# Decay gates from one product of 96 stacked rows in place of a plain float32 product of 16 rows

## The chip, the core and the metric

The kernel runs on one core of a Trainium2 chip. The metric is the device time of one execution in microseconds (us); less is better. Each kernel's time is the median of several runs, and one further execution was recorded by the hardware profiler. In the profile PE is TensorE's matmul, PEld its weight load, DVE VectorE, ACT ScalarE, POOL GpSimd, and SP the engine whose queue issues the DMAs.

## What is computed

A block of a streaming encoder on 1024 tokens of 1024 channels, with 16 meta tokens ahead of them, all in float32: a norm, one wide projection, a pooling mixer and a chunked gated linear attention side by side, a gated merge, an output projection, and an MLP with a squared ReLU. The part that matters here is the decay gate of the attention. `lr` is the slice of 16 channels of the projection (`GLA_GATE_RANK`), and there are 256 key channels:

```
log_a = jax.nn.log_sigmoid((lr @ w_gate_up + b_gate).astype(jnp.float32)) / GLA_TAU
...
b = jnp.cumsum(ac, axis=2)
decay = jnp.exp(-jnp.abs(b[:, :, :, None, :] - b[:, :, None, :, :]))
```

So the product in question is (1024 + 16 tokens) x 16 by 16 x 256. It is small beside the other products, but its result goes through an exponential of a running sum.

## The kernel before, in words

**Operands.** The large products are split. An operand x is kept as a high part hi (x rounded to the matmul type `float32r`, written by ACT) and a low part lo = x - hi (written by DVE, also as `float32r`), and a product is the sum of three matmuls, hi*hi, hi*lo and lo*hi (`mm3`, lines 280 to 282, called line by line L280, L281, L282). The gate product alone is different: line 506 multiplies plain float32 operands, `wgu` (16 rows x 256, the gate weights) and the transposed `lr` (16 rows x 512 tokens, kept in the first 16 rows of the tile `gB`; 16 x 16 for the meta tokens, in `lrT_meta`).

**Order of the work.** PE's order is the order of the code. ACT, DVE, POOL and SP each run one queue in order too, but what stands where in it is decided by a scheduler when the program is built. The steps around the change are: `start` (norms, transposes and the value projection `v_tile`, whose weights lie in the tiles `vw`; at its end `lr_turn`, which transposes `lr` on PE and copies it out of PSUM on ACT), `pool_open` (frees the tiles of `start` and opens those of the next stage), and then, by the list at the end of `differences`, a0, d0, a1, d1, m0, a2, m1, a3, m2, k0, m3. Here a(g) is `a_block(g)`, the projection of pooling group g, 72 matmuls and three evacuations on ACT (L555); d(p) is `decays(p)`, the gate for half p of the key channels: three gate products (tokens 0 to 511, tokens 512 to 1023, meta), and for each ACT adds the bias while it takes the product out of PSUM (L507), then does absolute value, exponential and logarithm (L508 to L510), DVE finishes (L511), and ACT exponentiates (L520) before the result is stored; m(g) is `mix_block(g)`, the pooling sums on DVE, their split into `ph` (L574, L575), and six matmuls.

**PSUM banks.** Products go to banks that are handed out in turn by tag. `ms` has three banks. `lr_turn` takes all three, d0 takes all three, d1 takes all three, and m0 takes the next one for its first product, that is the bank that d1's first product had. A bank can be written again when its reader is done; for a gate product the reader is ACT's L507. The projections use the three banks of the tag `mm`.

**Weights of the projections.** `W1` is a ring of two slots. As soon as the last matmuls of a block have read a slot, ACT and DVE split the weights of the block after the next into it (L84, L85); the scheduler puts these ahead of the evacuations of the gate products in ACT's queue.

**Later.** In the merge (steps `yb_block` and `out_tile`, from about 460 us on) SP's queue loads gate and pooling rows (L1029, into tiles `o`, `t` and `c`) and weights (L118, through the staging tiles `raw`), DVE multiplies and adds them (L1080, L1081), and ACT and DVE split the result (L1084, L1085).

Of the kernel before, what the change touches and what calls it, by code (L numbers as in the profile page):

```python
# [7 lines left out]
F32 = mybir.dt.float32  # L8
F32R = mybir.dt.float32r
U8 = mybir.dt.uint8  # L10
ACT = mybir.ActivationFunctionType
ALU = mybir.AluOpType
AX = mybir.AxisListType

P = 128
D = 1024
SEQ = 1024
META = 16
KT = D // P
HALF = 512  # L20
# [76 lines left out]
class Raw:  # L97
# [11 lines left out]
    def load(self, ap, n):  # L109
        while any(self.slots[self.n % len(self.slots)] is t for t in self.held):  # L110
            self.n += 1
        self.last = self.slots[self.n % len(self.slots)]
        dst = self.last[:, :n]
        self.n += 1
        view = dst
        if len(ap.shape) == 3:
            view = dst.rearrange("p (a b) -> p a b", a=ap.shape[1])
        self.nc.sync.dma_start(view, ap)  # L118
        return dst
# [3 lines left out]
def kernel(  # L123
# [3 lines left out]
    nc = tc.nc  # L127
# [3 lines left out]
    w_gate_up, b_gate, gla_norm, w_gla_out, w_out = w_gate_up[0], b_gate[0], gla_norm[0], w_gla_out[0], w_out[0]  # L131
    norm_ffn, w_ff1, w_ff2 = norm_ffn[0], w_ff1[0], w_ff2[0]

    act, dve, pool, pe = nc.scalar, nc.vector, nc.gpsimd, nc.tensor
    left, right = Stack(tc, "left"), Stack(tc, "right")
# [18 lines left out]
    def bank(tag):  # L154
        if tag == "sc":
            sc_n[0] += 1
            return two("sc")[:, sc_n[0] % 2]
        return psp[tag].tile([P, 512], F32, name=f"b_{tag}", tag=tag)

    def two(tag):  # L160

        if tag in ("sc", "gs"):
            if tag not in wide:
                wide[tag] = psp[tag].tile([P, 2, 512], F32, name=f"b_{tag}", tag=tag)
            return wide[tag]
        return psp[tag].tile([P, 2, 512], F32, name=f"b_{tag}", tag=tag)
# [17 lines left out]
    gB = left.push("gB", [P, D], F32)  # L184
# [10 lines left out]
    stat = [tiny(16) for _ in range(4)]  # L195
    eps_t = tiny(1)
    pool.memset(eps_t, EPS)
    wgu = left.push("wgu", [16, 256], F32)
    metab = left.push("metab", [P, 5, 16], F32)
    lrT_meta = left.push("lrT_meta", [16, META], F32)  # L200
    raw = Raw(nc, [left.push(f"raw{i}", [P, D], F32) for i in range(2)])
    W1 = Ring(tc, raw, left.push("w1h", [P, 2, D], F32R), left.push("w1l", [P, 2, D], F32R), 2)
    left_ff = left.mark()
# [8 lines left out]
    def f32(ap):  # L212
        return ap.bitcast(F32)

    def col(v, n):
        return v.rearrange("(h p) -> p h", p=P)
# [87 lines left out]
    S, rings = {}, [W1]  # L304
# [44 lines left out]
    def buffer(key, depth, size=HALF, side=None):  # L349
        S[key] = (side or left).push(key, [P, depth, size], F32)  # L350
        S["n" + key], S["d" + key] = 0, depth

    def nxt(key):
        i = S["n" + key]
        S["n" + key] += 1
        return S[key][:, i % S["d" + key]]

    def halves():
        return [slice(h * HALF, (h + 1) * HALF) for h in range(2)]
# [3 lines left out]
    def ask_vw(i):  # L363
        vw_raw[i] = [
            raw.load(w_cols(C_V + i * 256 + j * P), D).rearrange("p (k c) -> p k c", k=KT) for j in range(2)
        ]
# [35 lines left out]
            nc.sync.dma_start(v_dram[i, t], o)  # L402

    def lr_turn():
        b = bank("ms")
        pe.transpose(b[:16, :16], S["lrtok"][:16, 8], ident[:16, :16])
        act.activation(lrT_meta, b[:16, :16], ACT.Copy)
        for h in range(2):
            b = bank("ms")
            for t in range(4):  # L410
                pe.transpose(b[:16, t * P : (t + 1) * P], S["lrtok"][:, 4 * h + t], ident)
            act.activation(gB[:16, h * HALF : (h + 1) * HALF], b[:16], ACT.Copy)


    SPREAD = {
# [7 lines left out]
    def start():  # L423
        act.preload_act_table_set("natural_log_exp_and_others")
        xs = left.push("xs", [P, 4, D], F32)
        us = left.push("us", [P, 3, D], F32)
        S["lrtok"] = left.push("lrtok", [P, 10, 16], F32)
        S["lrraw"] = left.push("lrraw", [P, KT, 16], F32)
        xm = left.push("xm", [META, D], F32)
        um = left.push("um", [META, D], F32)  # L430
        mf = left.push("mf", [P, 6, CH], F32)
        S["xr"] = right.push("xr", [P, KT, SEQ], F32)
        S["vw"] = [right.push(f"vw{i}", [P, 2, KT, n], F32R) for i, n in enumerate((VP, 256))]
        buffer("vo", 3, 2 * P, right)
        load = lambda t: nc.sync.dma_start(xs[:, t % 4], x[t * P : (t + 1) * P, :])
        blank = S["xr"].rearrange("p k c -> p (k c)")[:, -640:]
        pool.memset(blank, 0.0)

        def warm(n, cols=HALF):
            for _ in range(n):  # L440
                pe.matmul(bank("ms")[:, :cols], blank[:, HALF:], blank[:, :cols], start=True, stop=True)

        load(0)
        nc.sync.dma_start(um[:1], norm_mix[None, :])
        nc.sync.dma_start(ident, ident_in)
        ask_vw(0)
        nc.sync.dma_start(S["lrraw"], w_in[:, C_LR : C_LR + 16].rearrange("(k p) c -> p k c", p=P))
        pool.memset(xm[:1, :P], 1.0)
        warm(2)
        for c in halves():  # L450
            b = bank("mm")
            pe.matmul(b, xm[:1, :P], um[:1, c], start=True, stop=True)
            dve.tensor_copy(gB[:, c], b)
        warm(2)
        for t in range(8):
            if 0 < t < 6:
                load(t + 2)
            if t == 1:
                nc.sync.dma_start(xm, meta)
            if t == 3:  # L460
                W1.top_up()
            u = us[:, t % 3]
            layer_norm(xs[:, t % 4], u)
            transposed(u, t // 4, OFF[t // 4] + (t % 4) * P, ("ms", "sc"))
            if t == 0:
                load(1)
                load(2)
                warm(10, P)
                load_vw(0)
                ask_vw(1)  # L470
            if t == 6:
                layer_norm(xm, um)
            if t == 1:
                warm(6, P)
            if t == 2:
                load_vw(1)
            if t < 3:
                v_tile(0, t)
            else:
                for i, n in SPREAD[t]:  # L480
                    v_tile(i, n)
        transposed(um, 0, 0)
        v_tile(0, 7)
        v_tile(1, 6)
        v_tile(1, 7)
        v_tile(0, 8)
        v_tile(1, 8)
        lr_turn()
        nc.sync.dma_start(mf, masks)
        pool.tensor_copy(mask, mf)  # L490
        nc.sync.dma_start(pscale, col(pool_scale, 4))
        nc.sync.dma_start(bgate, col(b_gate, 2))
        nc.sync.dma_start(gnorm, col(gla_norm, 4))
        nc.sync.dma_start(wgu, w_gate_up)

    one = []
    step(one, start)


# [3 lines left out]
    def log_decay(lrT, p, n, y, t):  # L503

        b = bank("ms")[:, :n]
        pe.matmul(b, wgu[:, p * P : (p + 1) * P], lrT, start=True, stop=True)
        act.activation(y, b, ACT.Identity, bias=bgate[:, p : p + 1])  # L507
        act.activation(t, y, ACT.Abs)  # L508
        act.activation(t, t, ACT.Exp, scale=-1.0)
        act.activation(t, t, ACT.Ln, bias=1.0)  # L510
        dve.scalar_tensor_tensor(y, y, 0.0, t, ALU.min, ALU.subtract)  # L511

    META_LOG = (0, 3)

    def decays(p):
        def fn():
            for half, c in enumerate(halves()):
                y = nxt("c")
                log_decay(gB[:16, c], p, HALF, y, nxt("t1"))
                act.activation(y, y, ACT.Exp, scale=1.0 / TAU)  # L520
                nc.sync.dma_start(decay_dram[p, half], y)
                yield 0.6
            if p:
                act.activation(gnorm, gnorm, ACT.Copy, scale=0.5)
            log_decay(lrT_meta, p, META, metab[:, META_LOG[p]], metab[:, 4])
            if p:
                tc.keep_in_program_order(act.preload_act_table_set("exp_and_others"))

        return fn

    def pool_open():
        left.pop_to(base)
        right.pop_to(1)
        buffer("c", 4)
        buffer("t1", 3)
        S["left_t"] = left.mark()
        buffer("a", 2, 1056)
        buffer("s", 2, 1056)
        S["ph"] = left.push("ph", [P, 2, SEQ], F32R)
        mw = S["mw"] = left.push("mw", [P, 2, 4, P], F32R)  # L540
        r = raw.load(w_pool_mix.rearrange("g c e -> c g e"), 4 * P).rearrange("p (g e) -> p g e", g=4)
        act.activation(mw[:, 0], r, ACT.Copy)
        dve.tensor_tensor(mw[:, 1], r, f32(mw[:, 0]), ALU.subtract)

    step(one, pool_open)

    pooled = {}
# [1064 lines left out]
```

## Time and profile before

| | us |
|---|---|
| runs of the kernel | 1223.77, 1224.25, 1226.83 (median 1224.25) |
| profiled execution | 1226.16 |
| its span, first to last instruction | 1224.0 |
| PE busy in the span | 1209.7 |
| DVE busy | 841.4 |
| ACT busy | 574.3 |
| POOL busy | 75.8 |

The profiled execution's own time is 2.2 us above its span, and 1.9 us above the median of the runs. A row of the timeline gives start, duration, engine, line, operation, output<-inputs and how many instructions were merged; in brackets stand the idle time before and what ended it. Matmuls overlap: a matmul of 512 columns is shown with 0.39 us, but the next one starts 0.23 us later. So the cost of matmuls is read from the distance of their starts, not from their durations.

### The profile page before, as it was taken

The numbers are of one execution on the slowest core, as the hardware profiler recorded it, in microseconds if no ns is written. First come the engines' busy times: TensorE is split into PE (matmuls) and PEld (weight loads), VectorE is DVE, ScalarE is ACT, GpSimd is POOL, SyncE is SP. The second block draws the span as 40 slices with busy tenths as digits, with TensorE's granted clock in tenths as the row PEclk, the third lists the DMA queues.
The fourth block names the chain that finished last, engine by engine and source line by source line (L and its number), as shares of the span: only waits on it lengthen the run. The fifth ranks groups of instructions, "written<-read, shape, count | busy, mean of one in ns | idle before, by whom it ended". The sixth has DMA issues, their size and how long they took to land.

```text
span 1224.0 us, 18376 instructions
## 1 busy us (share of the span) xinstructions
PE 1209.7 (99%) x6807; PEld 998.3 (82%) x6807; DVE 841.4 (69%) x1383; ACT 574.3 (47%) x1011; POOL 75.8 (6%) x96
## 2 busy tenths in 40 slices
PE   9999999999999999999999999999999999999997
PEld 6988987778778887888778888888888888888886
DVE  6535657665777568835887676676775887887686
ACT  7627444444456223413655455454554444444544
POOL 0000043222230000000000000000000000000000
PEclk9999999999999999999999999999999999999999
DMA  8312334435238976921245354444569973333532
GB/s 236 93 40 95 118 100 130 146 105 164 82 135 269 336 242 217 322 93 53 109 138 167 129 172 146 157 155 135 176 223 328 333 251 100 100 95 95 169 96 88
DMA packets 154411, 193.80 MB, mean 158 GB/s; under 512 B 12209, under 2 KB 89281, under 8 KB 154322
## 3 DMA queue, kind: packets, MB, share of 16 engines
q1 hardware_dynamic: 154322, 192.64, 48.6%
q8 instruction: 53, 0.87, 0.3%
q14 instruction: 36, 0.29, 0.1%
HBM read 129.67 MB, written 62.93 MB: 157 GB/s over the span
## 4 chain that ended last, share of the span: by engine, by line
PE 91%; DVE 3%; DMA 2%; ACT 1%; issue 1%; POOL 0%; SPq 0%; DVEq 0%; POOLq 0%; ACTq 0%
PE b_mm L282 7%; PE b_mm L280 7%; PE b_mm L281 7%; PE b_y L280 6%; PE b_y L281 6%; PE b_y L282 6%; PE b_oa L282 5%; PE b_oa L280 5%; PE b_oa L281 5%; PE b_z L280 4%; PE b_z L281 4%; PE b_z L282 4%; PE b_sc L280 4%; PE b_ob L282 4%; PE b_ob L280 4%; PE b_ob L281 4%
## 5 line engine op out<-in xcount | busy, mean ns | idle before, releaser
L677 ACT ACTIVATE w1h<-raw 128x512 fp32r<-128x512 f32 x106 | 65.9, 622 | 59.4 <-PE b_y L281 25.3
L678 DVE TENSOR_TENSOR w1l<-raw,w1h 128x512 fp32r<-128x512 f32 x106 | 72.5, 685 | 21.9 <-ACT w1h L677 21.9
L280 PE MATMUL b_sc<-th,w1h 128*128 128x512 f32 x216 | 85.6, 396 | 0.5 <-ACT u2p L1395 0.5
L280 PE MATMUL b_z<-th,w1h 128*128 128x512 f32 x216 | 85.2, 395 | 0.2 <-DVE c L796 0.2
L281 PE MATMUL b_sc<-tl,w1h 128*128 128x512 f32 x216 | 84.9, 393 | 0.0
L281 PE MATMUL b_z<-tl,w1h 128*128 128x512 f32 x216 | 84.3, 390 | 0.4 <-DVE tl L1283 0.4
L677 ACT ACTIVATE w1h<-fs 128x512 fp32r<-128x512 f32 x81 | 51.1, 631 | 71.0 <-PE b_y L281 33.4
L282 PE MATMUL b_sc<-th,w1l 128*128 128x512 f32 x216 | 84.4, 391 | 0.0
L282 PE MATMUL b_z<-th,w1l 128*128 128x512 f32 x216 | 84.1, 389 | 0.0
L678 DVE TENSOR_TENSOR w1l<-fs,w1h 128x512 fp32r<-128x512 f32 x81 | 57.0, 704 | 26.6 <-ACT w1h L677 26.5
L280 PE MATMUL b_mm<-th,w1h 128*128 128x512 f32 (+1 forms) x208 | 72.1, 347 | 0.0
L281 PE MATMUL b_mm<-tl,w1h 128*128 128x512 f32 (+1 forms) x208 | 71.0, 342 | 0.0
L282 PE MATMUL b_mm<-th,w1l 128*128 128x512 f32 (+1 forms) x208 | 71.0, 341 | 0.0
L677 ACT ACTIVATE w1h<-bt 128x512 fp32r<-128x512 f32 x46 | 29.1, 632 | 70.8 <-issue 43.9
L1471 DVE TENSOR_TENSOR bt<-w,w 128x512 f32<-128x512 f32 x80 | 54.7, 684 | 0.4 <-DMA w<-in_w_ff_dram 0.4
L280 PE MATMUL b_mm<-wo,th 128*128 128x512 f32 x128 | 50.4, 394 | 0.0
L282 PE MATMUL b_mm<-wo,tl 128*128 128x512 f32 x128 | 49.9, 390 | 0.0
L281 PE MATMUL b_mm<-wo,th 128*128 128x512 f32 x128 | 49.8, 389 | 0.0
L280 PE MATMUL b_y<-wo,w1h 128*128 128x512 f32 x128 | 49.8, 389 | 0.0
L281 PE MATMUL b_y<-wo,w1h 128*128 128x512 f32 x128 | 49.8, 389 | 0.0
L282 PE MATMUL b_y<-wo,w1l 128*128 128x512 f32 x128 | 49.8, 389 | 0.0
L678 DVE TENSOR_TENSOR w1l<-bt,w1h 128x512 fp32r<-128x512 f32 x46 | 31.8, 691 | 25.6 <-ACT w1h L677 25.6
(405 smaller groups left out, 3342.7 us busy)
## 6 DMA issues: line engine op xcount, KB each, us to landing
hf_dram<-h SPq DMA_DIRECT2D x112, 256.0 KB, 2.1
raw<-hf_dram SPq DMA_DIRECT2D x112, 256.0 KB, 2.7
w<-in_w_ff_dram SPq DMA_DIRECT2D x64, 256.0 KB, 4.5
raw<-in_w_in_dram SPq DMA_DIRECT2D x22, 512.0 KB, 4.6
raw<-in_w_ff_dram SPq DMA_DIRECT2D x16, 512.0 KB, 4.2
rawx<-in_w_ff_dram SPq DMA_DIRECT2D x16, 512.0 KB, 4.2
rawp<-in_w_in_dram SPq DMA_DIRECT2D x10, 512.0 KB, 4.2
xs<-in_x_dram SPq DMA_DIRECT2D x8, 512.0 KB, 4.7
```

The source lines that it names most:

```text
L280: pe.matmul(ps, ah, bh, start=first and i == 0, stop=False, skip_group_check=more)
L281: pe.matmul(ps, ah, bl, start=False, stop=False, skip_group_check=more)
L282: pe.matmul(ps, al, bh, start=False, stop=last and i == n - 1, skip_group_check=more)
L677: act.activation(hi, a, ACT.Copy)
L678: dve.tensor_tensor(lo, a, f32(hi), ALU.subtract)
L1471: dve.tensor_tensor(bt, w, S["w2"][q[3:]][:, i], ALU.add if q[2] == "+" else ALU.subtract)
```

## The change

The gate product becomes one matmul in the split form, with the three terms laid under one another in the 128 rows of the array. Two new tiles of 96 rows are made, `lr` (96 x 1040) and `gu` (96 x 256), both `float32r`. In `lr`, rows 0 to 15 and 64 to 79 hold hi of the transposed `lr`, rows 32 to 47 hold lo. In `gu`, rows 0 to 15 and 32 to 47 hold hi of the gate weights, rows 64 to 79 hold lo. All other rows are zero. One product over the 96 rows is then hi*hi + lo*hi + hi*lo.

For this the weights are loaded three times into `wgu`, which now has 96 rows and is cleared by POOL at the start; `lr` is cleared by POOL; `stacked` writes hi twice on ACT and lo once on DVE for each of the three pieces; `gu` takes one ACT and one DVE instruction. `lr_turn` is called from `pool_open` and no longer from `start`. The tiles `lr` and `gu` lie where `vw` was.

```
-    wgu = left.push("wgu", [16, 256], F32)
+    wgu = left.push("wgu", [96, 256], F32)
...
-    lrT_meta = left.push("lrT_meta", [16, META], F32)
...
     def lr_turn():
+        def stacked(to, b):
+            act.activation(to[:16], b, ACT.Copy)
+            act.activation(to[64:80], b, ACT.Copy)
+            dve.tensor_tensor(to[32:48], b, f32(to[:16]), ALU.subtract)
+
         b = bank("ms")
         pe.transpose(b[:16, :16], S["lrtok"][:16, 8], ident[:16, :16])
-        act.activation(lrT_meta, b[:16, :16], ACT.Copy)
-        for h in range(2):
+        stacked(S["lr"][:, SEQ:], b[:16, :16])
+        for h, c in enumerate(halves()):
             b = bank("ms")
             for t in range(4):
                 pe.transpose(b[:16, t * P : (t + 1) * P], S["lrtok"][:, 4 * h + t], ident)
-            act.activation(gB[:16, h * HALF : (h + 1) * HALF], b[:16], ACT.Copy)
+            stacked(S["lr"][:, c], b[:16])
...
         pool.memset(blank, 0.0)
+        pool.memset(wgu, 0.0)
...
-        lr_turn()
         nc.sync.dma_start(mf, masks)
...
-        nc.sync.dma_start(wgu, w_gate_up)
+        for r in (0, 32, 64):
+            nc.sync.dma_start(wgu[r : r + 16], w_gate_up)
...
-        pe.matmul(b, wgu[:, p * P : (p + 1) * P], lrT, start=True, stop=True)
+        pe.matmul(b, S["gu"][:, p * P : (p + 1) * P], lrT, start=True, stop=True)
...
-                log_decay(gB[:16, c], p, HALF, y, nxt("t1"))
+                log_decay(S["lr"][:, c], p, HALF, y, nxt("t1"))
...
-            log_decay(lrT_meta, p, META, metab[:, META_LOG[p]], metab[:, 4])
+            log_decay(S["lr"][:, SEQ:], p, META, metab[:, META_LOG[p]], metab[:, 4])
...
     def pool_open():
+        right.pop_to(1)
+        S["lr"] = right.push("lr", [96, SEQ + META], F32R)
+        S["gu"] = right.push("gu", [96, 256], F32R)
+        pool.memset(f32(S["lr"]), 0.0)
+        lr_turn()
+        act.activation(S["gu"], wgu, ACT.Copy)
+        dve.tensor_tensor(S["gu"][64:96], wgu[64:], f32(S["gu"][64:96]), ALU.subtract)
         left.pop_to(base)
-        right.pop_to(1)
```

PE's order stays what it was, matmul for matmul; only the gate products read other tiles. At d1, PE stands so before (b_ms is a bank of the tag `ms`, th and w1l are operands of a1, ph and mw those of m0):

```order
L282 MATMUL b_mm<-th_144,w1l 128x512
L506 MATMUL b_ms<-gB,wgu 128x512 x2
L506 MATMUL b_ms<-lrT_meta,wgu 128x16
L280 MATMUL b_ms<-ph,mw 128x512
L281 MATMUL b_ms<-ph,mw 128x512
L282 MATMUL b_ms<-ph,mw 128x512
```

And now, where the lines of the code have moved (L506 is L511, L280 to L282 are L279 to L281):

```order
L281 MATMUL b_mm<-th_140,w1l 128x512
L511 MATMUL b_ms<-lr,gu 128x512 x2
L511 MATMUL b_ms<-lr,gu 128x16
L279 MATMUL b_ms<-ph,mw 128x512
L280 MATMUL b_ms<-ph,mw 128x512
L281 MATMUL b_ms<-ph,mw 128x512
```

The first matmul of m0, into a bank of `ms`, still stands right behind the three gate products of d1.

ACT's queue around `lr_turn` before (L542 splits the mix weights, L398 evacuates the last value tiles, L607 belongs to `differences`, L555 evacuates a0, L507 takes d0's gate products out of PSUM):

```order
L542 ACTIVATE mw<-raw_120 128x512
L398 ACTIVATE gB<-b_mm 16x256 x2
L407 ACTIVATE lrT_meta<-b_ms 16x16
L607 ACTIVATE t2h<-xr 128x2048
L412 ACTIVATE gB<-b_ms 16x512 x2
L555 ACTIVATE a<-b_mm 128x264 x2
L84 ACTIVATE w1h<-raw_124 128x1024
L555 ACTIVATE a<-b_mm 128x512
L507 ACTIVATE c<-b_ms,small 128x512 x2
```

And now:

```order
L542 ACTIVATE gu<-wgu 96x256
L397 ACTIVATE gB<-b_mm 16x256 x2
L405 ACTIVATE lr<-b_ms 16x16
L406 ACTIVATE lr<-b_ms 16x16
L618 ACTIVATE t2h<-xr 128x2048
L405 ACTIVATE lr<-b_ms 16x512
L406 ACTIVATE lr<-b_ms 16x512
L405 ACTIVATE lr<-b_ms 16x512
L406 ACTIVATE lr<-b_ms 16x512
L566 ACTIVATE a<-b_mm 128x264 x2
L84 ACTIVATE w1h<-raw_120 128x1024
L566 ACTIVATE a<-b_mm 128x512
```

Four instructions of ACT are added ahead of a0's first evacuation; behind it, through d1, L84 still stands ahead of the evacuation of the gate products.

Far from the change, in the merge, the scheduler's order of SP's queue comes out differently. Before (raw are staging tiles for weights, o and t the tiles of gate and pooling rows):

```order
L118 DMA raw_120<-in_w_gla_out_dram 128x4x256
L1029 DMA o<-gb_dram 128x512
L1029 DMA o<-ma_dram 128x512
L1029 DMA o<-gb_dram 128x512
L1029 DMA o<-ma_dram 128x512
L1029 DMA t_4717<-gb_dram 128x512
L1029 DMA t_4717<-ma_dram 128x512
L1029 DMA t_4717<-gb_dram 128x512
L1029 DMA t_4717<-ma_dram 128x512
L118 DMA raw_124<-in_w_gla_out_dram 128x4x256
```

And now:

```order
L118 DMA raw_116<-in_w_gla_out_dram 128x4x256
L118 DMA raw_120<-in_w_gla_out_dram 128x4x256
L1040 DMA t_4735<-gb_dram 128x512
L1040 DMA t_4735<-ma_dram 128x512
L1040 DMA t_4735<-gb_dram 128x512
L1040 DMA t_4735<-ma_dram 128x512
L1040 DMA o<-gb_dram 128x512
L1040 DMA o<-ma_dram 128x512
L1040 DMA o<-gb_dram 128x512
L1040 DMA o<-ma_dram 128x512
```

The second load of weights has moved ahead of the eight loads of rows, and the `t` loads ahead of the `o` loads. At d0 a few small rows of ACT and DVE have changed places; between d1 and the merge the order of ACT, DVE and SP is the same as before.

## Prediction, made before the changed kernel was run

> **What bounds the kernel now.** The page first: the span, the busy time of the engines and the shares of the chain that ended last.
>
> ```profile
> span 1224.0 us, 18376 instructions
> ...
> PE 1209.7 (99%) x6807; PEld 998.3 (82%) x6807; DVE 841.4 (69%) x1383; ACT 574.3 (47%) x1011; POOL 75.8 (6%) x96
> ...
> PE 91%; DVE 3%; DMA 2%; ACT 1%; issue 1%; POOL 0%; SPq 0%; DVEq 0%; POOLq 0%; ACTq 0%
> ```
>
> PE is idle for 14 of 1224 us, and 91% of the chain is PE. A microsecond taken from PE's queue is therefore worth a microsecond, if PE doesn't then stand still for something else. Next the chain in order of time, at the gate products (start, length, what):
>
> ```profile
> 91.50 2.04 PE b_ms L506 x6
> 105.07 2.04 PE b_ms L506 x6
> ```
>
> Both groups of gate products, d0 and d1, lie on the chain with 2.04 us each. PE's timeline at d0 and at d1 gives the finer picture:
>
> ```profile
> 90.66 0.39 PE L280 MATMUL b_mm<-th,w1h 128*128 128x512 f32 x1
> 90.89 0.39 PE L281 MATMUL b_mm<-tl,w1h 128*128 128x512 f32 x1
> 91.11 0.39 PE L282 MATMUL b_mm<-th,w1l 128*128 128x512 f32 x1
> 91.43 1.98 PE L506 MATMUL b_ms<-gB,wgu 16*128 16x512 f32 x4
> 93.25 0.28 PE L506 MATMUL b_ms<-lrT_meta,wgu 16*128 16x16 f32 x2
> 93.47 0.39 PE L280 MATMUL b_mm<-th,w1h 128*128 128x264 f32 x1
> 93.69 0.28 PE L281 MATMUL b_mm<-tl,w1h 128*128 128x264 f32 x1
> 93.81 0.28 PE L282 MATMUL b_mm<-th,w1l 128*128 128x264 f32 x1
> ...
> 104.46 0.39 PE L281 MATMUL b_mm<-tl,w1h 128*128 128x512 f32 x1
> 104.69 0.39 PE L282 MATMUL b_mm<-th,w1l 128*128 128x512 f32 x1
> 105.00 1.98 PE L506 MATMUL b_ms<-gB,wgu 16*128 16x512 f32 x4
> 106.83 0.29 PE L506 MATMUL b_ms<-lrT_meta,wgu 16*128 16x16 f32 x2
> 107.11 0.47 PE L280 MATMUL b_ms<-ph,mw 128*128 128x512 f32 x1
> ```
>
> A `float32r` matmul of 512 columns takes 0.225 us from start to start (90.66, 90.89, 91.11). A plain float32 product of 512 columns is two instructions; four of them and the first meta instruction fill 91.43 to 93.25, so one product costs about 0.86 us, nearly four times as much. It uses 16 rows of the array, and nothing in these rows says that fewer rows are cheaper.
>
> **The change, part by part.** *d0.* Without gate products the next matmul would start at 91.11 + 0.225 = 91.34; it starts at 93.47. The step costs 2.13 us. Now it is two products at 0.225 and one of 16 columns, for which I take 0.12, the distance at which matmuls of 264 columns follow each other (93.69, 93.81): 0.57 us. Bounds for that last one are 0 and 0.225. What follows is a1: its weights have been in the other slot since `start`, and its banks are of another tag. So d0 gives back 2.13 - 0.57 = 1.56, about 1.6 us (1.45 to 1.7).
>
> *d1.* The same sum at d1 is 107.11 - (104.69 + 0.225) = 2.20 us against 0.57, again 1.6 us on PE. But next is m0, which needs the bank of d1's first product. ACT's rows at d1:
>
> ```profile
> 104.89 1.06 ACT L84 ACTIVATE w1h<-raw 128x1024 fp32r<-128x1024 f32 x1 [2.38 <-PE b_mm L281]
> 105.85 0.58 ACT L555 ACTIVATE a<-b_mm 128x512 f32<-128x512 f32 x1
> 106.33 1.39 ACT L507 ACTIVATE c<-b_ms,small 128x512 f32<-128x512 f32 x2
> ```
>
> ACT starts the weights' split L84 when PE's last reader of that slot is done (the L281 from 104.46, shown to 104.85), then evacuates a1, and only then takes the gate product out: two L507 in 1.39 us, so the first is done at 106.33 + 0.69 = 107.02. PE's next start was 107.11, by its own sum and by ACT's alike: the two paths ended together. ACT's path hangs on the end of a1 and none of its three steps gets shorter, and its order at this place is unchanged. So m0 still starts 2.2 us behind the end of a1. How soon PE follows ACT is seen later, where it waits for ACT:
>
> ```profile
> 478.51 1.04 ACT L84 ACTIVATE w1h<-raw 128x1024 fp32r<-128x1024 f32 x1
> ...
> 479.61 0.50 PE L280 MATMUL b_mm<-yg,w1h 128*128 128x512 f32 x1 [2.33 <-ACT w1h L84]
> ...
> 480.94 0.80 PE L282 MATMUL b_mm<-yg,w1l 128*128 128x512 f32 x1 [0.60 <-DVE w1l L85]
> ```
>
> 478.51 + 1.04 to 479.61 is 0.06 us, so m0 could come at 107.08 instead of 107.11: a gain of 0.03, taken as 0. The new wait of about 1.6 us stands at m0's first matmul; behind it in PE's queue stand m0's other five and a2, and ACT and DVE wait for those. Its other operand, `ph`, comes from
>
> ```profile
> 100.68 0.69 DVE L575 TENSOR_TENSOR ph<-s,ph 128x512 fp32r<-128x512 f32 x1
> ```
>
> at 101.4, still ahead of 107.1 - 1.6 = 105.5.
>
> *Preparation.* ACT and DVE around `lr_turn`:
>
> ```profile
> 81.47 1.04 ACT L412 ACTIVATE gB<-b_ms 16x512 f32<-16x512 f32 x2
> 83.18 0.39 ACT L555 ACTIVATE a<-b_mm 128x264 f32<-128x264 f32 x1 [0.67 <-PE b_mm L282]
> ...
> 81.60 2.29 DVE L608 TENSOR_TENSOR t2l<-xr,t2h 128x2048 fp32r<-128x2048 f32 x1 [4.13 <-ACT t2h L607]
> 92.40 1.23 DVE L85 TENSOR_TENSOR w1l<-raw,w1h 128x1024 fp32r<-128x1024 f32 x1 [8.51 <-ACT w1h L84]
> ```
>
> ACT has four pieces of 512 in place of two, 1.04 us more, and a small one more; with 0.67 us free it delays a0's first evacuation by about 0.5 us, and that bank is next written in a1, at 92. The split of `gu`, one more, falls into ACT's idle time ahead of 79. DVE makes the low parts behind t2l (to 83.9), two of at most 0.69 us: done by 85.4. d0 needs them at 91.34, so 6 us cover them; and DVE has 8.5 us free there. Uncovered, all of it would cost 2.5 us. ACT's `gu` and POOL's clearing of `lr` must wait until `vw` has been read, by
>
> ```profile
> 76.05 0.29 PE L282 MATMUL b_mm<-vw,tl 128*16 128x272 f32 x1
> ...
> 0.77 0.63 POOL L437 MEMSET xr<- 128x640 f32 x1
> 33.83 0.50 SPq L494 DMA_DIRECT2D wgu<-in_w_gate_up_dram  x1
> ```
>
> at 76.34. POOL cleared 640 columns in 0.63 us, so 1040 take about 1.0: done at 77.4, two microseconds ahead of the transposes' evacuation at 79.6. Clearing `wgu` (0.25 us) stands at the start on an idle POOL. Two more DMA issues of 0.50 us each delay the weights of a2 on SP from 35.4 to 36.4, and a2's split reads them at 91. All this is counted at nothing.
>
> *Sum.* 1.56 + 0.03 + 0 = 1.6 us off. The profiled execution's 1226.16 would become 1224.6; it lies 1.9 above the median, and the median goes from 1224.25 to **1222.6**. Behind m0 I expect everything 1.6 us earlier in the same order, the merge apart.
>
> **The rivals.** *Both steps pay* (3.2 us, 1221.0): if ACT took d1's product out ahead of L84. The order says no; the bank's turn could be misread. 0.12.
>
> *The clock trips at m0.* Where PE had stood still, its clock was halved (granted clock is the column after POOL):
>
> ```profile
> 477.00:481.00 4.00, 1.07 (x5) 0.36 (x3) 4.00 (x7) 2.10 (x3) 0.00 (x0) 1.00 0.84 274
> 481.00:484.40 3.40, 3.40 (x8) 2.72 (x9) 1.78 (x3) 1.58 (x2) 0.00 (x0) 0.50 0.97 351
> 490.00:600.00 110.00, 109.50 (x504) 90.22 (x503) 66.21 (x112) 40.30 (x72) 0.00 (x0) 1.00 0.42 148
> ```
>
> Gaps of 2.33 and 0.60 us were followed by 3.4 us at 0.50, a loss of 1.7. A new gap of 1.6 might do the same: 1222.6 + 1.7 = 1224.3. [...] The trace thus speaks against leaning on it, but half as long a gap is milder: 0.13.
>
> *The wait at 477 shrinks.* It is fed by loads and stores whose landing varies, as in the answer on L1029:
>
> ```profile
> DMA to landing us min/median/max: 2.6/4.4/7.3
> ```
>
> If only the halved clock is escaped, 1222.6 - 1.7 = 1220.9; if the gaps go too, 2.9 more: 1218.0. The change does nothing for it. 0.10.
>
> *Slower: the moved loads of the merge.* Four loads into `o` now stand behind a load of weights and four into `t`:
>
> ```profile
> 489.92 1.22 DVE L85 TENSOR_TENSOR w1l<-raw,w1h 128x1024 fp32r<-128x1024 f32 x1
> ...
> 487.87 0.34 SPq L1029 DMA_DIRECT2D o<-gb_dram  x1
> 493.56 0.43 SPq L118 DMA_DIRECT2D raw<-in_w_gla_out_dram  x1
> ...
> 500.43 0.68 DVE L1080 SCALAR_TENSOR_TENSOR o<-o,b_mm 128x512 f32<-128x512 f32 x1
> ```
>
> The weights' staging tile is free at 491.2, so the first `o` load slips from 487.87 to about 493.6, and its reader runs at 500.43: 6.9 us, enough for the median landing and just short of enough for the slowest. But 0.5 MB and five loads of 0.26 MB, 1.8 MB, go out from 491.2; at the stage's mean of 148 GB/s they land at 503.4, 2.9 us late, and PE would wait for the bank: 1222.6 + 2.9 = 1225.5, slower. It decides against the kernel below 1.8 MB in 9.2 + 1.6 = 10.8 us, 167 GB/s; the queue ran at 274 and 351 where it was loaded, so 0.10.
>
> *The 96 rows cost as much as float32 before* (no gain, 1224.25): nothing speaks for it, as a `float32r` matmul of 128 rows has 0.225 us. 0.05.
>
> **How the numbers follow.** The forecast has 0.50. Runs differ by 3.1 us (1223.77 to 1226.83), so each case is smeared by about 1.5 us. The range 1219.8 to 1225.7 takes in forecast, both steps, clock, moved loads and no gain, and the nearer half of the shrunken wait. A measurement can tell about 0.3%, 3.7 us: faster means below 1220.6, which is the wait at 477 shrinking (0.10) and a third of both steps (0.04), 0.14 together. Slower means above 1227.9: a quarter of the moved loads and of the clock (0.06). Within 0.3%: 0.80.
>
> **What would show it.** Right: d0 takes about 0.6 us on PE; m0's first matmul shows an idle time of about 1.6 us that ACT's L507 ends (L512 there); a2 starts 1.6 us earlier than before, not 3.2; DVE's low parts are done by 86; the clock stays at 1.00 around 105. Wrong: m0 without a wait; a wait at d0; a clock of 0.50 behind m0; PE waiting for DVE or a DMA between 485 and 515; or a wait near 477 that has changed by more than a microsecond.

## The result and the profile after

| | us |
|---|---|
| before, 6 runs beside the changed kernel | 1225.46 median (1222.6 to 1226.86) |
| changed kernel, 6 runs | 1230.01 median (1229.53 to 1232.73) |
| ratio to before | 1.0044 [1.003, 1.0057] |
| profiled execution of the changed kernel | 1231.92, span 1230.0 |
| predicted | 1222.6 (1219.8 to 1225.7) |

The kernel became 0.44% slower, about 5 us, where 1.6 us of gain were forecast; the time lies above the range. The page of the changed kernel:

```profile
span 1230.0 us, 18382 instructions
...
PE 1212.6 (99%) x6801; PEld 997.0 (81%) x6801; DVE 843.9 (69%) x1387; ACT 576.1 (47%) x1015; POOL 77.1 (6%) x98
```

PE has six instructions fewer (the three gate products were x6 at d0 and at d1, and are x3 now) and is busy 2.9 us longer, and the span is 6.0 us longer, so PE's idle time grew by 3.1 us. The idle time is about that of three new waits, read below (1.50, 0.86 and 0.68 us). The busy time is the surprise: the gate products became about 3.2 us shorter, so the rest of PE's work takes about 6 us longer.

**The gate products.** PE's timeline of the changed kernel at d0 and d1 (L511 is the gate product, L279 to L281 the projections, before called L280 to L282):

```profile
90.77 0.39 PE L281 MATMUL b_mm<-th,w1l 128*128 128x512 f32 x1
90.99 0.64 PE L511 MATMUL b_ms<-lr,gu 96*128 96x512 f32 x3
91.49 0.37 PE L279 MATMUL b_mm<-th,w1h 128*128 128x264 f32 x1
...
102.69 0.39 PE L281 MATMUL b_mm<-th,w1l 128*128 128x512 f32 x1
102.91 0.64 PE L511 MATMUL b_ms<-lr,gu 96*128 96x512 f32 x3
105.06 0.50 PE L279 MATMUL b_ms<-ph,mw 128*128 128x512 f32 x1 [1.50 <-ACT c L512]
```

The three products of d0 take 91.49 - (90.77 + 0.225) = 0.50 us, where they took 2.13. At d1 they are as short, but m0 starts at 105.06, 2.14 us behind the end of a1 (2.20 before), after 1.50 us of waiting for ACT. ACT at the same place:

```profile
102.88 1.06 ACT L84 ACTIVATE w1h<-raw 128x1024 fp32r<-128x1024 f32 x1 [0.66 <-PE b_mm L280]
103.85 0.58 ACT L566 ACTIVATE a<-b_mm 128x512 f32<-128x512 f32 x1
104.33 1.26 ACT L512 ACTIVATE c<-b_ms,small 128x512 f32<-128x512 f32 x2
```

The chain is the one foretold: split of the weights, evacuation of a1, evacuation of the gate product, then m0. The preparation on ACT, DVE and POOL:

```profile
83.77 0.39 ACT L566 ACTIVATE a<-b_mm 128x264 f32<-128x264 f32 x1
...
83.81 1.28 DVE L407 TENSOR_TENSOR lr<-b_ms,lr 16x512 fp32r<-16x512 f32 x2
...
76.07 0.96 POOL L540 MEMSET lr<- 96x1040 f32 x1 [40.93 <-PE b_mm L281]
```

a0's first evacuation is 0.59 us later than before, the low parts are done at 85.09, and `lr` is cleared at 77.03; no PE wait follows from any of them. The step that the change is about does what was said of it.

**Where the time went.** Here are matmuls that stand in both kernels, from PE's timeline before:

```profile
93.47 0.39 PE L280 MATMUL b_mm<-th,w1h 128*128 128x264 f32 x1
...
485.15 0.39 PE L281 MATMUL b_mm<-yg,w1h 128*128 128x512 f32 x1
...
495.89 0.50 PE L280 MATMUL b_mm<-yg,w1h 128*128 128x512 f32 x1
...
631.23 0.47 PE L280 MATMUL b_z<-th,w1h 128*128 128x512 f32 x1
...
896.29 0.39 PE L282 MATMUL b_sc<-th,w1l 128*128 128x512 f32 x1
...
1203.20 0.39 PE L280 MATMUL b_oa<-w1h,fxh 128*128 128x512 f32 x1
```

and the same ones in the changed kernel (the first of them is the row at 91.49 above):

```profile
483.78 0.46 PE L280 MATMUL b_mm<-yg,w1h 128*128 128x512 f32 x1
...
495.63 0.51 PE L279 MATMUL b_mm<-yg,w1h 128*128 128x512 f32 x1 [0.86 <-DVE t L1091]
...
632.25 0.47 PE L279 MATMUL b_z<-th,w1h 128*128 128x512 f32 x1 [0.68 <-DVE h L1423]
...
898.60 0.39 PE L281 MATMUL b_sc<-th,w1l 128*128 128x512 f32 x1
...
1209.09 0.39 PE L279 MATMUL b_oa<-w1h,fxh 128*128 128x512 f32 x1
```

After minus before: -1.98, -1.37, -0.26, +1.02, +2.31, +5.89 us. Of the lead of 1.98 us behind d0, 0.35 was there ahead of d0. Between 178 and 350 us 0.7 us of it go, nearly all by 184 us, at two waits of 0.23 and 0.44 us that were 0 and 0.24 before. In the merge 1.1 us go at a new wait for DVE, and up to 632 us another 1.3, of which 0.68 is a further new wait. From 631 us on, through the MLP, the difference grows by 4.9 us without any wait. The windows view tells it in counts (two stretches of the MLP, first before, then after; the first number in brackets is PE's matmuls):

```profile
640.00:880.00 240.00, 240.00 (x1061) 198.72 (x1060) 169.34 (x265) 121.86 (x204) 0.00 (x0) 1.00 0.47 154
930.00:1200.00 270.00, 270.00 (x1192) 223.56 (x1192) 208.38 (x348) 122.06 (x223) 0.00 (x0) 1.00 0.51 165
```

```profile
640.00:880.00 240.00, 240.00 (x1055) 197.72 (x1055) 168.43 (x264) 120.68 (x201) 0.00 (x0) 1.00 0.47 154
930.00:1200.00 270.00, 270.00 (x1179) 220.87 (x1178) 205.85 (x340) 120.71 (x220) 0.00 (x0) 1.00 0.52 166
```

PE is never idle in either kernel, the granted clock is 1.00, and yet 6 and 13 matmuls fewer start in the same time. From the starts of single matmuls of 512 columns in the trace (distances above 260 ns left out): 226.7 ns apart before in both stages, now 227.8 ns from 620 to 900 us and 229.4 ns from 915 to 1210 us. About 1240 matmuls x 1.1 ns and 1300 x 2.7 ns make 1.4 + 3.5 = 4.9 us, the whole drift.

By operands, the slowest are those that take one operand from each side of the memory: tiles are pushed on a left side that grows upwards (`w1h`, `th`, `wo` and others) or a right side that grows downwards (`fxh`, `t4h`, `yg` and others). Pairs of `w1h` and `fxh` went from 226.3 to 233 ns; pairs of `wo` and `w1h`, both left, stayed at 226.7. But matmuls with both operands on one side have a part in it: in the last stage, behind each switch of sides, most of the first ten are slower (single ones up to 236 ns), and from the eleventh on they are back at 226 to 227. By the means, about 1.5 of the last stage's 3.5 us fall on them. The line of the diff that reaches them is the removal of `lrT_meta`, 16 columns of 4 bytes: it moved every left-side tile pushed behind it down by 64 bytes, and no right-side tile. In the built program `w1h` starts at byte 31616 of each partition before and at 31552 now, `fxh` at 219008 in both. By 256, the large operand tiles of both sides had the remainder 128 before; now the left ones have 64.

### The profile page after: what moved, and what is told of

Its sections match the earlier page's. It is cut to its first block, busy times and chain, and to the rows that moved or that the text cites. A ratio compares the mean times of both kernels' runs of the same rounds, so it can differ in the third digit from the quotient of the medians.

```text
span 1230.0 us, 18382 instructions
## 1 busy us (share of the span) xinstructions
PE 1212.6 (99%) x6801; PEld 997.0 (81%) x6801; DVE 843.9 (69%) x1387; ACT 576.1 (47%) x1015; POOL 77.1 (6%) x98
## 4 chain that ended last, share of the span: by engine, by line
PE 91%; DVE 4%; DMA 2%; issue 2%; ACT 1%; POOL 0%; SPq 0%; DVEq 0%; ACTq 0%; POOLq 0%
PE b_mm L279 7%; PE b_mm L281 7%; PE b_mm L280 7%; PE b_y L279 6%; PE b_y L280 6%; PE b_y L281 6%; PE b_oa L281 5%; PE b_oa L279 5%; PE b_oa L280 5%; PE b_z L279 4%; PE b_z L280 4%; PE b_z L281 4%; PE b_sc L279 4%; PE b_ob L279 4%; PE b_ob L281 4%; PE b_ob L280 4%
## 5 line engine op out<-in xcount | busy, mean ns | idle before, releaser
L279 PE MATMUL b_sc<-th,w1h 128*128 128x512 f32 x216 | 86.0, 398 | 0.7 <-ACT u2p L1406 0.5
L279 PE MATMUL b_z<-th,w1h 128*128 128x512 f32 x216 | 85.3, 395 | 1.1 <-DVE h L1423 0.7
L280 PE MATMUL b_sc<-tl,w1h 128*128 128x512 f32 x216 | 84.7, 392 | 0.0
L280 PE MATMUL b_z<-tl,w1h 128*128 128x512 f32 x216 | 84.3, 390 | 0.4 <-DVE tl L1294 0.4
L281 PE MATMUL b_sc<-th,w1l 128*128 128x512 f32 x216 | 84.7, 392 | 0.0
L281 PE MATMUL b_z<-th,w1l 128*128 128x512 f32 x216 | 84.1, 390 | 0.0
L279 PE MATMUL b_mm<-th,w1h 128*128 128x512 f32 (+1 forms) x208 | 72.0, 346 | 0.0
L280 PE MATMUL b_mm<-tl,w1h 128*128 128x512 f32 (+1 forms) x208 | 71.1, 342 | 0.0
L281 PE MATMUL b_mm<-th,w1l 128*128 128x512 f32 (+1 forms) x208 | 71.0, 341 | 0.0
L279 PE MATMUL b_mm<-wo,th 128*128 128x512 f32 x128 | 50.6, 395 | 0.0
L281 PE MATMUL b_mm<-wo,tl 128*128 128x512 f32 x128 | 50.1, 391 | 0.0
L280 PE MATMUL b_mm<-wo,th 128*128 128x512 f32 x128 | 49.8, 389 | 0.0
L279 PE MATMUL b_y<-wo,w1h 128*128 128x512 f32 x128 | 49.8, 389 | 0.0
L280 PE MATMUL b_y<-wo,w1h 128*128 128x512 f32 x128 | 49.8, 389 | 0.0
L281 PE MATMUL b_y<-wo,w1l 128*128 128x512 f32 x128 | 49.8, 389 | 0.0
```

The costliest lines, as they stand in the source:

```text
L279: pe.matmul(ps, ah, bh, start=first and i == 0, stop=False, skip_group_check=more)
L280: pe.matmul(ps, ah, bl, start=False, stop=False, skip_group_check=more)
L281: pe.matmul(ps, al, bh, start=False, stop=last and i == n - 1, skip_group_check=more)
```

## The experiments

Two losses were to be explained, the drift and the merge, and a gain that stays behind the wait at m0. The theory: the drift comes from the distance between the addresses of the two operands, the merge from another order there, and neither from the gate product. The rival: something in the new step (its tiles, its work on ACT, DVE, POOL or SP) slows PE later on.

**e1: the 64 bytes put back.**

```
     metab = left.push("metab", [P, 5, 16], F32)
+    left.push("fill", [P, 16], F32)
```

> The changed kernel with an unused tile of 64 bytes per partition in the place of the tile lrT_meta that the change took away, so that every tile behind it has its address of before again; the scheduler's order in the merge is then the one of before too. Address theory (the loss comes from the 64 bytes by which the tiles of the left side moved): matmuls of 512 columns are 226.7 ns apart again in both parts of the MLP (they were 227.8 and 229.4 in the changed kernel), no PE wait near 495, m0's wait of 1.5 us stays, and the time is 1.6 us below the kernel before (1.0 to 2.2). Rival (the loss comes from the stacked product itself or from its preparation, or from the new wait at m0 by way of the clock or of later transfers): the time stays 4 to 5 us above the kernel before.

Measured: 1222.29 us against 1226.39 before, ratio 0.9981 [0.9969, 0.9993]; span 1219.3. By the ratio that is 2.3 us below before, a little more than the 1.0 to 2.2 expected, but the interval (0.9 to 3.8) takes them in. The two MLP stretches:

```profile
640.00:880.00 240.00, 240.00 (x1060) 198.79 (x1060) 170.38 (x267) 123.26 (x205) 0.00 (x0) 1.00 0.47 154
930.00:1200.00 270.00, 270.00 (x1193) 223.65 (x1192) 209.66 (x351) 121.88 (x222) 0.00 (x0) 1.00 0.50 159
```

Counts and distances (226.7 ns) are those of before, and the wait for `t`, now at 491 us, is 0.2 us, where none was expected. The gate product with 96 rows is kept, so it isn't what costs.

**e2: the kernel before, moved by 64 bytes.** The float32 gate product stays; `lrT_meta` goes into unused bytes at the other edge of the memory.

```
-    edge.push("pad", [P, 24], F32)
+    edge_pad = edge.push("pad", [P, 24], F32)
...
-    lrT_meta = left.push("lrT_meta", [16, META], F32)
+    lrT_meta = edge_pad[:16, :META]
```

> The kernel before with its plain float32 gate product, in which only lrT_meta is moved into an unused tile at the other end of the memory, so that the tiles of the left side lie 64 bytes lower, as in the changed kernel; the scheduler then makes the merge's order of the changed kernel. Address theory: slower than the kernel before by 6.1 us (5 to 7.5), that is by the changed kernel's loss of 4.5 and the 1.6 that d0 gave it; MLP matmuls 227.8 and 229.4 ns apart; PE waits near 495. Rival (the stacked product): no difference from the kernel before.

Measured: 1230.88 us, ratio 1.005 [1.0032, 1.0067].

```profile
640.00:880.00 240.00, 240.00 (x1055) 197.75 (x1054) 169.28 (x265) 121.32 (x202) 0.00 (x0) 1.00 0.47 154
930.00:1200.00 270.00, 270.00 (x1179) 220.86 (x1178) 207.07 (x346) 120.94 (x222) 0.00 (x0) 1.00 0.52 163
```

The counts of the changed kernel, without any of its new work; PE also waits 0.85 us for `t` in the merge. The rival falls: 64 bytes alone cost what the kernel lost, and more.

**e3: the changed kernel, right-side tiles moved 64 bytes up.** The distance between the sides has then changed by 128 bytes against before.

```
-    edge.push("pad", [P, 24], F32)
+    edge.push("pad", [P, 8], F32)
```

> The changed kernel in which the unused tile at the right end has 32 bytes instead of 96, so that the tiles of the right side lie 64 bytes higher and both sides have the same remainder by 128 again, 64 in place of 0. All queues have the order of the changed kernel. Theory of the difference (a matmul is slowed when the operands that are read at the same time lie at different remainders by 128): MLP matmuls 226.7 ns apart, the wait near 495 stays, 5.0 us faster than the changed kernel, so about 0.5 us below the kernel before. Theory of alignment (an operand off the grid of 128 bytes is itself slow): all MLP matmuls now slow, 229 to 233 ns, no faster than the changed kernel and up to 6 us slower.

Measured: 1230.08 us, ratio 1.0046 [1.0029, 1.0062].

```profile
930.00:1200.00 270.00, 270.00 (x1178) 220.92 (x1177) 205.52 (x340) 120.70 (x220) 0.00 (x0) 1.00 0.52 166
```

Nothing is healed (227.8 and 229.5 ns). So it isn't the remainder by 128 bytes that must agree. The other theory on record, that an operand off the grid of 128 bytes is slow by itself, isn't met either: pairs of `wo` and `w1h`, both off that grid, stay at 226.7. Left were a distance with a longer period (theory A with 256 bytes, theory B with 1024, in the expectations below) and the left side's place by itself (theory C).

**e4: e1, and m0's first product into a bank of the tag `mm`.**

```
-            for h, (tag, c) in enumerate(zip(("ms", "sc"), halves())):
+            for h, (tag, c) in enumerate(zip(("mm", "sc"), halves())):
```

> The kernel of the first experiment, in which the first product of each mix block takes its bank from the tag of the projections (mm) and no longer from the gates' (ms), so that m0 need not wait until ACT has taken d1's first product out. Theory (d1's saving is swallowed by the wait for the bank): no wait at m0, a2 starts 1.5 us earlier than in the first experiment, and the time is 3.1 us below the kernel before (2.4 to 3.8). Rival (something behind m0 is late anyway, ACT's queue above all): the same time as the first experiment.

Measured: 1223.06 us, ratio 0.9979 [0.9968, 0.9991], not to be told from e1. PE's timeline:

```profile
103.44 0.64 PE L512 MATMUL b_ms<-lr,gu 96*128 96x512 f32 x3
103.94 0.48 PE L280 MATMUL b_mm<-ph,mw 128*128 128x512 f32 x1
...
177.57 0.50 PE L280 MATMUL b_sc<-th,w1h 128*128 128x512 f32 x1 [0.58 <-ACT u2p L800]
...
477.62 0.50 PE L280 MATMUL b_mm<-yg,w1h 128*128 128x512 f32 x1 [2.33 <-ACT w1h L84]
```

m0 follows without a wait, 0.50 us behind the start of the gate products (1.50 us of waiting in the changed kernel, 1.51 in e1), which shows that the bank was what held it at d1. Against e1, matmul by matmul, 1.7 us are gained at m0, 0.4 of them are lost at 177 us at a wait of 0.58 us (0.15 in e1), and 1.2 last to 476 us. Behind that, this execution lost 1.2 us to e1 around a stretch at a lower granted clock (0.63 from 477 to 481 us and 0.93 from 481 to 484.4, where that of e1 has 1.00), and it had lost 2.6 us to e1 in the first 22 us, where the edit touches nothing. So the spans can't be compared, and whether 1.2 us reach the end can't be told from the medians either: the 1.5 us that the expectation sets between e1 and e4 are not shown in the times.

**e5 to e8, e10, e11: the distance alone, in the last product.** On e1, an unused tile pushes `fxh` and `fxl` down in the last product of the MLP; every engine's order and every earlier address are those of e1. The diff is that of e5 (16 columns, 64 bytes); e6, e7, e8, e10 and e11 have 32, 64, 128, 48 and 8 columns.

```
         S["bt"] = right.push("bt", [P, 2, HALF], F32)
+        right.push("fill2", [P, 16], F32)
```

> The kernel of e1 (left-side tiles back where they were before), but in the last product of the MLP alone the two right-side tiles fxh and fxl lie 64 bytes lower; every engine's order is that of e1. Theory A (the distance between the two operands of a matmul counts, as a remainder): the matmuls of 512 columns in the last stage, from 915 to 1210 us, start 228.5 to 230.5 ns apart in the mean instead of 226.7, pairs of one left and one right operand 230 to 233.5, and the stages before stay at 226.7; the span is 2 to 4.5 us above that of e1 as far as the half-clock stretches are alike. Theory C (the place of the left-side tiles alone counts): 226.7 in every stage, the span of e1.

> As e5 with 128 bytes. Theory A with a period above 128 bytes: 228.5 to 230.5 ns in the last stage, like the 229.5 of e3, in which the distance had also changed by 128 bytes. Theory C: 226.7, since no left-side tile is moved.

> As e5 with 256 bytes. Theory A with a period of 256 bytes: 226.7 ns again. Theory B (a period of 1024 bytes, all distances before having been multiples of 1024 or nearly all): 228 ns or more. Theory C: 226.7.

> As e5 with 512 bytes. Theory A with a period of 256 or 512 bytes: 226.7 ns. Theory B (1024 bytes): 228 ns or more. Theory C: 226.7.

> The kernel of e1 with fxh and fxl 192 bytes lower in the last product. With a period of 256 bytes, 192 lower is as 64 higher, the distance that the changed kernel has: from 915 to 1210 us 229.2 to 229.5 ns between the starts in the mean, and by pairs the pattern of the changed kernel (w1h over fxl 233, fxl over w1h 228), not that of e5 (233 the other way round). Without a period, some value between those of 128 and 256 bytes, below 229.

> The kernel of e1 with fxh and fxl 32 bytes lower in the last product. If it is the offset within a unit of 64 bytes that counts too, 228 ns or more; if only whole units of 64 bytes count, 226.7. No theory so far tells which; a guess is a loss of a similar size to that of 64 bytes.

Each had one execution. The stretch from 930 to 1200 us, with 64 bytes (e5):

```profile
930.00:1200.00 270.00, 270.00 (x1179) 220.87 (x1178) 207.14 (x347) 120.76 (x220) 0.00 (x0) 1.00 0.51 162
```

128 bytes (e6):

```profile
930.00:1200.00 270.00, 270.00 (x1178) 220.90 (x1177) 206.84 (x347) 120.70 (x220) 0.00 (x0) 1.00 0.51 162
```

256 bytes (e7):

```profile
930.00:1200.00 270.00, 270.00 (x1193) 223.58 (x1192) 209.04 (x350) 122.55 (x224) 0.00 (x0) 1.00 0.51 161
```

512 bytes (e8):

```profile
930.00:1200.00 270.00, 270.00 (x1193) 223.65 (x1192) 209.66 (x352) 121.88 (x222) 0.00 (x0) 1.00 0.50 160
```

192 bytes (e10):

```profile
930.00:1200.00 270.00, 270.00 (x1178) 220.85 (x1178) 207.44 (x346) 120.88 (x222) 0.00 (x0) 1.00 0.51 160
```

32 bytes (e11):

```profile
930.00:1200.00 270.00, 270.00 (x1175) 220.29 (x1174) 205.72 (x344) 120.61 (x220) 0.00 (x0) 1.00 0.51 163
```

Mean distance of the starts, worked out from the same traces (ns; the last two columns are the distance from a matmul of this pair of operands to the next, as the profile names the pairs):

| left against right, bytes | 620 to 900 us | 915 to 1210 us | w1h,fxl | fxl,w1h |
|---|---|---|---|---|
| 0 (e1) | 226.7 | 226.7 | 226.9 | 226.9 |
| -64 (changed kernel) | 227.8 | 229.4 | 233.3 | 228.1 |
| +192 (e10) | 226.7 | 229.4 | 233.3 | 228.3 |
| +64 (e5) | 226.7 | 229.4 | 231.5 | 233.4 |
| +128 (e6) | 226.7 | 229.6 | 233.5 | 231.7 |
| +32 (e11) | 226.7 | 230.1 | 233.7 | 233.3 |
| +256 (e7) | 226.7 | 226.7 | 226.8 | 226.9 |
| +512 (e8) | 226.7 | 226.7 | 226.5 | 227.1 |

The single executions took 1227.48 (e5), 1226.98 (e6), 1222.52 (e7), 1221.34 (e8), 1225.65 (e10) and 1230.66 us (e11). These times hold more than the distance: e5's span is 6.3 us above e1's, where 2 to 4.5 were expected, and 2.8 of it arise in the first 22 us. Matmul by matmul e5 loses 3.5 us to e1 between 900 and 1200 us, and e7 and e8 lose none there.

The loss switches on and off in the one stage whose distance was touched (226.7 or 229.4 to 230.1 ns), with the left side untouched: the distance counts, not the left side's place. 256 and 512 bytes cost nothing (226.7 ns), so of the periods put forward that of 256 bytes fits all eight rows. And 192 bytes give, pair by pair, the figures of -64 bytes (233.3 and 228.3 ns beside 233.3 and 228.1), as a period of 256 demands. The period of 1024, by which e7 should have 228 ns or more, falls with its 226.7.

**e9: the order of the merge alone.** With 64 bytes less the merge's tile `o` overlaps an older tile `o`; the scheduler then waits with its loads and places other work of SP and DVE ahead. Here the overlap is taken away, and the left-side tiles elsewhere stay 64 bytes lower, as in the changed kernel.

```
         S["left2"] = left.mark()
+        left.push("fillm", [P, 16], F32)
```

> The changed kernel, its left-side tiles still 64 bytes lower than before, except that in the merge the tiles t1, o and raw3 are put back to their old addresses by 64 unused bytes. So o no longer overlaps the older tile o, every engine's order is that of e1, and the loss by distance stays. Two causes, one each: if the changed order in the merge costs something, the wait of PE for DVE's t at 495 us is gone and this kernel runs 0.8 to 1.7 us under the changed kernel's 1230.0, at about 1228.5, 1.0024 of the time before; the matmuls of 512 columns in the MLP stay at 227.8 and 229.4 ns. If the order costs nothing, about 1230.0. If order were all and the distance nothing, 1222 to 1223, as e1.

Measured: 1229.74 us, ratio 1.003 [1.0019, 1.0042]. DVE in the changed kernel around the wait of PE:

```profile
493.76 1.22 DVE L85 TENSOR_TENSOR w1l<-raw,w1h 128x1024 fp32r<-128x1024 f32 x1
494.90 0.68 DVE L1091 SCALAR_TENSOR_TENSOR t<-t,b_mm 128x512 f32<-128x512 f32 x1
```

and in e9, with PE's row behind it:

```profile
494.99 0.69 DVE L1091 SCALAR_TENSOR_TENSOR t<-t,b_mm 128x512 f32<-128x512 f32 x1
495.59 1.22 DVE L85 TENSOR_TENSOR w1l<-raw,w1h 128x1024 fp32r<-128x1024 f32 x1
...
495.77 0.46 PE L279 MATMUL b_mm<-yg,w1h 128*128 128x512 f32 x1
```

The built program has DVE's order changed here as well as SP's. In the changed kernel DVE comes to this place earlier, but splits weights for 1.22 us before it reads the bank that PE needs; so PE waits 0.86 us. In e9 that wait is gone, and between 419 and 496 us the changed kernel loses 1.1 us against e9. It loses another 0.9 at 632 us, where its wait for `h` (0.68 us) is absent in e9; e3 has this wait too, e2 has not, so it doesn't follow from the order alone. ACT's rows, first of the changed kernel, then of e9, show what DVE waited for:

```profile
630.15 0.63 ACT L688 ACTIVATE w1h<-raw 128x512 fp32r<-128x512 f32 x1 [3.62 <-DMA raw<-in_w_ff_dram]
...
629.18 0.63 ACT L688 ACTIVATE w1h<-raw 128x512 fp32r<-128x512 f32 x1 [2.54 <-DMA raw<-in_w_ff_dram]
```

The loads of these weights were issued at the same time (from 624.72 and 624.69 us), and the one that ACT needs landed 1 us later. Why it did stays open; one execution of each can't tell whether the change has a part in it. The drift is there as before (227.8 and 229.4 ns). The medians of e9 and of the changed kernel differ by 0.3 us and their ratios by 1.7 us, with intervals that overlap: that the order costs about 1 us is shown in the traces, not in the times.

## Why the prediction was wrong

- **d0, 1.56 us:** right. The step takes 0.50 us, not 0.57, and gives 1.63.
- **d1, no gain:** right. m0 waits 1.50 us, ended by L512, and e4 shows that the turn of the bank was the reason. The rival by which both steps pay falls.
- **Preparation, nothing:** right in each term: 0.59 us for a0's evacuation (0.5 foretold), 85.09 us for the low parts (85.4), 77.03 for POOL (77.4).
- **The clock at m0:** it didn't trip; around the idle 1.50 us the granted clock, from 93 to 107 us, is 1.00. That half as long a gap is milder was the author's estimate. No run shows a length of gap from which the clock falls: behind 2.33 and 0.60 us it was 0.50 in the kernel before, and behind 2.32 and 0.60 us 1.00 in e1.
- **The moved loads of the merge:** their late landing, priced at 2.9 us, isn't what happened; what cost 1.1 us there was the place of L85 ahead of L1091 on DVE. The list of signs had it ("PE waiting for DVE or a DMA between 485 and 515"), the sum hadn't.
- **The step that failed:** "Behind m0 I expect everything 1.6 us earlier in the same order, the merge apart." It took for granted that a matmul behind m0 takes as long as before. The removed tile `lrT_meta` was read as a buffer that is gone, not as 64 bytes that carried the address of all left-side tiles behind it. That term, absent from the sum and from the rivals, is 4.9 us of drift in the MLP. With the merge's 1.1 us and the 0.7 us at 632 us it outweighs the gain.

The forecast's own sum is borne out by e1 only in part. The change without the shift has a ratio of 0.9981 [0.9969, 0.9993], which is 0.9 to 3.8 us of 1226, and 1.6 lies inside. In its trace d0 gives 1.66 us, but 0.7 of them are gone again by 470 us, as in the changed kernel, so "1.6 us earlier" didn't hold ahead of the merge either. The rest of the 4.7 us between the two spans is not the change: 2.5 us are the first 22 us, and about 1.6 the clock behind the gaps at 477 (0.50 from 481.0 to 484.4 us before, 1.00 in e1).

Why the distance counts isn't shown. In the last stage of e2 and e5 the starts lie 2.7 ns further apart (229.4 against 226.7), but no run here tests a cause; the mechanism stays open.

## What to carry to other kernels

Where tiles are pushed one behind the other, adding or removing a small one moves all that follow: compare the addresses of the large operands before and after, and the order of the queues where tiles now overlap, before reading anything else into a time. In this kernel the `float32r` matmuls of 512 columns in the last stage started 226.7 ns apart where the left and the right tiles had the same remainder by 256 bytes, and 229.4 to 230.1 ns apart at the other distances tried; a filler of 64 bytes was worth more (ratio 0.9981 with it, 1.0044 without) than the change itself (1.6 us at d0). The slowdown of the MLP, without waits and at a granted clock of 1.00, showed in the count of matmuls per stretch (1179 against 1192 from 930 to 1200 us), not in the busy share, which is 100% in both.

## What the runs showed of the hardware that wasn't expected

- In the last stage the `float32r` matmuls of 512 columns with operands on both sides (`w1h` and `fxl`) were followed by the next one after 226.5 to 227.1 ns (means by pair) where the distance was the old one or 256 or 512 bytes off it (e1, e7, e8), and after 228.1 to 233.7 ns at 32, 64, 128 and 192 bytes (e11, the changed kernel and e5, e6, e10). In the changed kernel matmuls whose two operands lie on one side lost less (at most 3.7 ns in the mean of a pair, `fxh` on `fxh` from 226.3 to 230.0), and mainly near a switch of sides: among the first ten behind it, single ones up to 236 ns.
- The halved clock behind the gaps at 477 us isn't a fixed consequence of them. In e1 the gaps are the same (2.32 and 0.60 us), and PE runs at 1.00 where the kernel before ran at 0.50, with 16 matmuls in the stretch from 481.0 to 484.4 us in place of 8 (15 at the place of the same matmuls, 477.6 to 481.0):

```profile
476.19 0.50 PE L280 MATMUL b_mm<-yg,w1h 128*128 128x512 f32 x1 [2.32 <-ACT w1h L84]
...
477.52 0.51 PE L282 MATMUL b_mm<-yg,w1l 128*128 128x512 f32 x1 [0.60 <-DVE w1l L85]
...
481.00:484.40 3.40, 3.40 (x16) 2.82 (x16) 2.94 (x4) 1.31 (x2) 0.00 (x0) 1.00 0.75 238
```

By 3.4 us at 0.50 in place of 1.00, this moves a single execution by about 1.7 us.
- The first microseconds differ too. Four matmuls at 5 us take 3.78 us in the kernel before and 1.98 us in e1:

```profile
5.17 3.78 PE L452 MATMUL b_mm<-um,xm 1*128 1x512 f32 x4
...
4.99 1.98 PE L458 MATMUL b_mm<-um,xm 1*128 1x512 f32 x4
```

By 22 us e1 is 2.5 us ahead. The edits aren't the reason: e4 and e5 are the same program as e1 up to there, and they begin like the kernel before, as do the changed kernel and e9; the other runs are nearer to e1. What decides it isn't shown. Both effects together are over 4 us, so the spans of single executions can't be compared as wholes, and they are compared stretch by stretch here.
